# One list of steps for the seven-product blocks and the down projection of a feed-forward block

## The chip, the cores and the metric

The kernel runs on one core of one Trainium2 chip. The metric is device time in microseconds (us) of one execution; three executions of the kernel before gave 2733.2, 2736.87 and 2738.81 us, median 2736.87. A further execution was profiled; the rows below are of that one.

## The reference

The program is one hybrid layer (dilated attention beside a gated linear recurrence) followed by a block of two layers, each made of a feed-forward block, a token mixer and a second feed-forward block, over 512 tokens of width 1024. Everything is float32. What the change touches is a feed-forward block:

```python
D_MODEL, SEQ, D_FF = 1024, 512, 2816
def _swiglu(h, w_gate, w_up, w_down):
    return (jax.nn.silu(h @ w_gate) * (h @ w_up)) @ w_down
...
h = _rmsnorm(x, norm_g[l, 0]) * (1.0 + sc0) + sh0
x = x + 0.5 * g0 * _swiglu(h, ffn_w_gate[l, 0], ffn_w_up[l, 0], ffn_w_down[l, 0])
```

There are four such blocks. The first one is computed by another function (`ffn`), the other three by `ffn7`, so the change touches three stages of the program.

## The kernel before

All float32 products are made of three products of parts: `split` (L390 to L400) writes the rounded high half of an operand on ScalarE (ACT, L399) and the rest, the low half, on VectorE (DVE, L400); TensorE (PE) then multiplies high by high, low by high and high by low.

In `ffn7`, the 22 column blocks (of 128) of the hidden width are taken in pairs. The first two pairs of blocks (0 to 3) are computed in the plain way. The other nine pairs (blocks 4 to 21) use seven products where the plain way has eight: gate and up weights of 256 columns, each cut into two halves of 512 rows, are a two by two matrix of pieces A11, A12 (gate), A21, A22 (up); the normed input, cut by rows and by tokens, is the other one. In the code A11 and A12 are the two halves of a `raw` tile, A21 and A22 are `pc` tiles. Each product (`prod`) is 24 matmuls at L1385, each with 256 columns. In order the seven are called here by their second operand: b11 and b21 (in `begin`), then t2, t1, t3, b22 and t4 (in `rest`). b11, t2, t3 and t4 add up in one PSUM bank (`acc`), which ScalarE copies out in between (L1399, L1417, L1427); t1 and b22 share another bank (`att`), which is copied out once (L1424).

Three of the left operands are sums that VectorE makes first, in place: A21+A22 in two halves (L1411), A21+A11 (L1412), A11 plus the first sum (L1414, in two halves) and A12 plus that (L1428). t2 multiplies what L1414 left in the `raw` tile, so its split needs both of them done. When all products of a pair are there, L1436 to L1441 make the activation (tanh on ScalarE, products and halves) into `sm` and `pT` tiles, and `down` multiplies the activations of two pairs with four column parts of the down weights (L1454, 24 matmuls of 512 columns for each part) and adds them to x (L1259).

A block runs `begin` of the first pair, `down` of the pass before, `rest`, and then `begin` and `rest` of the second pair with no `down` between. The passes are blocks 4 to 7, 8 to 11, 12 to 15, then 16 and 17 alone (one pair, and its `down` half as long), then 18 to 21, whose down projection is in `tail`. So in each of the three stages there are four places where a pair's `begin` is followed at once by its `rest`: pairs 6, 10, 14 and 20.

What sets the order: each engine has a list of instructions that it runs one after the other. A scheduler lays the lists out before the run, from the dependencies, from the order in which the program issues the work (earlier first) and from when tiles come free. `hi` and `lo` have 4 buffers each, `raw` 2, the pieces (`piece`, L1336) 3, the accumulators `acc` 2 and `att` 6. Loads are issued on SyncE's queue (SP).

Of the kernel before, what the change touches and what calls it, by code (L numbers as in the profile page):

```python
# [8 lines left out]
F32 = mybir.dt.float32  # L9
# [285 lines left out]
class Prog:  # L295
# [1047 lines left out]
    def ffn7(self, l, s, h, nxt):  # L1343
# [44 lines left out]
        class Pair:  # L1388
            pass

        def begin(f):

            u = Pair()
            u.cs = slice(f * 128, f * 128 + 256)
            u.raw = self.wload([(0, wg[:, u.cs])], KD, 256)
            u.a = self.acc()
            prod(u.a, both(u.raw[:, 0:4, :]), forms.b11, True)
            u.s1 = self.s()
            nc.scalar.activation(u.s1, u.a, AF.Copy)  # L1399
            b = self.att()  # L1400
            prod(b, both(u.raw[:, 4:8, :]), forms.b21, True)
            nc.vector.tensor_add(u.s1, u.s1, b)
            return u

        def rest(u, dst):
            u.p21, u.p22 = (self.piece(wu[a:a + 512, u.cs], 4) for a in (0, 512))
            a11, a12 = u.raw[:, 0:4, :], u.raw[:, 4:8, :]

            s1 = [self.s(shape=(128, 2, 256)) for _ in range(2)]
            for i in range(2):  # L1410
                nc.vector.tensor_add(s1[i], u.p21[:, 2 * i:2 * i + 2, :], u.p22[:, 2 * i:2 * i + 2, :])  # L1411
            nc.vector.tensor_add(u.p21, u.p21, a11)  # L1412
            for i in range(2):
                nc.vector.tensor_add(a11[:, 2 * i:2 * i + 2, :], a11[:, 2 * i:2 * i + 2, :], s1[i])  # L1414
            prod(u.a, both(a11), forms.t2, False)
            s2 = self.s()
            nc.scalar.activation(s2, u.a, AF.Copy)  # L1417
            c = self.att()
            hi, lo = (self.wp.tile([128, 4, 256], F32R, name=self.nm(n), tag=n) for n in ("hi", "lo"))
            for i in range(2):  # L1420
                self.split(s1[i], hi[:, 2 * i:2 * i + 2, :], lo[:, 2 * i:2 * i + 2, :])
            prod(c, (hi, lo), forms.t1, True)
            s5 = self.s()
            nc.scalar.activation(s5, c, AF.Copy)  # L1424
            prod(u.a, both(u.p21), forms.t3, False)
            s3 = self.s()
            nc.scalar.activation(s3, u.a, AF.Copy)  # L1427
            nc.vector.tensor_add(a12, a12, a11)  # L1428
            prod(c, both(a12), forms.b22, False)
            nc.vector.tensor_add(s3, s3, s5)  # L1430
            nc.vector.tensor_add(s2, s2, c)
            prod(u.a, both(u.p22), forms.t4, False)

            for hf, (g, up) in enumerate(((u.s1, u.a), (s2, s3))):
                t = self.s()
                nc.scalar.activation(t, g, AF.Tanh, scale=0.5)  # L1436
                nc.vector.scalar_tensor_tensor(t, t, 1.0, g, op0=ALU.add, op1=ALU.mult)
                nc.vector.tensor_mul(t, t, up)
                hi, lo = (d[:, hf].rearrange("p f n -> p (f n)") for d in dst)
                nc.scalar.activation(hi, t, AF.Copy, scale=-1.0)  # L1440
                nc.vector.scalar_tensor_tensor(lo, t, -1.0, hi.bitcast(F32), op0=ALU.mult, op1=ALU.subtract)  # L1441

        def down(f0, f1, aa):
            kc = f1 - f0
            for p in range(4):
                raw = self.piece(wd[f0 * 128:f1 * 128, p * 256:(p + 1) * 256], kc)
                hi, lo = (self.wp.tile([128, 4, 256], F32R, name=self.nm(n), tag=n)[:, 0:kc, :] for n in ("hi", "lo"))
# [660 lines left out]
```

## Time and profile before

| | |
|---|---|
| median of three executions | 2736.87 us |
| the profiled execution | 2743.27 us |
| its span, first to last instruction | 2741.5 us |
| mean granted TensorE clock | 0.986 of full speed |
| PE busy | 2625.5 us, 96% |
| DVE busy | 1978.6 us, 72% |
| ACT busy | 1168.8 us, 43% |

The profiled execution is 6.4 us (0.2%) above the median. Its time lies 1.8 us above its span. Busy means that an instruction of the engine was under way. A row of the chain, of the waits or of the time line says in the last place who ended the wait.

### The profile page before, as it was taken

Reading aid. Unit: us, or ns where it says so; the run is one execution under the profiler, and the core shown is the slowest. Engines: PE = TensorE matmul, PEld = TensorE weight load, DVE = VectorE, ACT = ScalarE, POOL = GpSimd, SP = SyncE. Lnnn points to the kernel's source line nnn. Section 1 sums busy time; section 2 is a strip of 40 time slices with the busy share of each in tenths; the row PEclk is TensorE's granted clock in tenths of the full one; section 3 lists DMA queues with packets and bytes.
Section 4 is the critical chain, followed back from the end, with each engine's and each line's share of the span. In section 5 each row is a group of like instructions: output and inputs, shape, how many; then the busy total and the mean of one; then the engine's idle time right before and its main releaser. Section 6 shows DMA issues by size and latency. Waiting matters only on the chain.

```text
span 2741.5 us, 40806 instructions
## 1 busy us (share of the span) xinstructions
PE 2625.5 (96%) x15952; PEld 2289.4 (84%) x15952; DVE 1978.6 (72%) x3401; ACT 1168.8 (43%) x2112; POOL 321.6 (12%) x425
## 2 busy tenths in 40 slices
PE   7999989999998999999999999999999999999998
PEld 6878767788787889887888888888889887888888
DVE  8776874845887546788777777777777688667776
ACT  5332342624322224547534435444444547434434
POOL 4010010103000002423200001000002413200001
PEclk9999999999999999999999999999999999999999
DMA  9867645232676333622133334133233522123321
GB/s 273 248 199 219 215 141 182 65 122 93 199 232 223 118 104 103 180 67 62 55 93 94 105 94 133 52 93 100 85 116 98 168 57 66 58 89 106 99 84 63
DMA packets 317233, 339.70 MB, mean 124 GB/s; under 512 B 22128, under 2 KB 287856, under 8 KB 317040
## 3 DMA queue, kind: packets, MB, share of 16 engines
q1 hardware_dynamic: 317040, 337.10, 40.4%
q8 instruction: 125, 2.05, 0.3%
q14 instruction: 68, 0.56, 0.1%
HBM read 328.67 MB, written 8.39 MB: 123 GB/s over the span
## 4 chain that ended last, share of the span: by engine, by line
PE 72%; DVE 12%; DMA 9%; issue 3%; ACT 2%; POOL 1%; SPq 0%; DVEq 0%; POOLq 0%; ACTq 0%
PE acc L1385 11%; PE att L1454 10%; PE att L1385 8%; DMA mraw<-in_w_ada 8%; PE acc L417 6%; PE acc L419 6%; PE acc L415 5%; DVE macc L656 3%; PE acc L467 2%; PE acc L573 2%; PE acc L577 2%; DVE lo L400 2%; PE acc L575 2%; PE att L1895 1%; PE att L1879 1%
## 5 line engine op out<-in xcount | busy, mean ns | idle before, releaser
L399 ACT ACTIVATE hi<-raw 128x1024 fp32r<-128x1024 f32 (+2 forms) x329 | 326.7, 994 | 484.9 <-PE acc L419 134.7
L400 DVE TENSOR_TENSOR lo<-raw,hi 128x1024 fp32r<-128x1024 f32 (+2 forms) x329 | 379.1, 1154 | 107.8 <-ACT hi L399 103.6
L1385 PE MATMUL acc<-s,hi 128*128 128x256 f32 x1728 | 261.0, 286 | 31.2 <-ACT hi L399 31.2
L415 PE MATMUL acc<-s,hi 128*128 128x512 f32 x1008 | 274.4, 407 | 15.8 <-ACT s L399 7.9
L417 PE MATMUL acc<-s,lo 128*128 128x512 f32 x1008 | 266.7, 400 | 0.0
L1385 PEld LDWEIGHTS acc<-s,hi 128*128 128x128 f32 x1728 | 233.2, 194 | 35.2 <-ACT hi L399 33.6
L419 PE MATMUL acc<-s,hi 128*128 128x512 f32 x1008 | 260.8, 395 | 0.0
L130 POOL TENSOR_TENSOR q<-q,q 128x256 f32<-128x256 f32 x96 | 79.8, 832 | 1531.3 <-ACT q L125 1529.4
L656 DVE SCALAR_TENSOR_TENSOR macc<-mraw,cs,macc 128x1024 f32<-128x1024 f32 x133 | 171.0, 1286 | 106.5 <-DMA mraw<-in_w_ada 102.7
L415 PEld LDWEIGHTS acc<-s,hi 128*128 128x128 f32 x1008 | 190.4, 192 | 62.2 <-ACT s L399 9.1
L417 PEld LDWEIGHTS acc<-s,lo 128*128 128x128 f32 x1008 | 192.4, 191 | 45.9 <-issue 0.5
L419 PEld LDWEIGHTS acc<-s,hi 128*128 128x128 f32 x1008 | 190.1, 189 | 43.7
L400 DVE TENSOR_TENSOR lo<-pc,hi 128x1024 fp32r<-128x1024 f32 (+1 forms) x138 | 156.3, 1134 | 80.0 <-ACT hi L399 79.7
L1385 PE MATMUL att<-s,hi 128*128 128x256 f32 x1296 | 197.1, 284 | 0.1
L399 ACT ACTIVATE hi<-pc 128x1024 fp32r<-128x1024 f32 (+1 forms) x138 | 135.1, 981 | 108.3 <-PE att L1454 52.9
L1385 PEld LDWEIGHTS att<-s,hi 128*128 128x128 f32 x1296 | 172.6, 191 | 1.6 <-ACT hi L399 1.6
L1454 PE MATMUL att<-sm,hi 128*128 128x512 f32 x528 | 146.4, 393 | 0.0
L1385 PE MATMUL acc<-s,lo 128*128 128x256 f32 x864 | 141.4, 287 | 4.3 <-DVE lo L400 4.3
L1259 DVE SCALAR_TENSOR_TENSOR x<-att,der,x 128x512 f32<-128x512 f32 x120 | 89.6, 749 | 66.8 <-PE att L1454 66.8
L1259 DVE SCALAR_TENSOR_TENSOR x<-acc,der,x 128x256 f32<-128x256 f32 (+1 forms) x136 | 76.0, 560 | 73.9 <-PE acc L577 48.8
L1385 PEld LDWEIGHTS acc<-s,lo 128*128 128x128 f32 x864 | 121.1, 194 | 4.9 <-DVE lo L400 4.9
L1454 PEld LDWEIGHTS att<-sm,hi 128*128 128x128 f32 x528 | 98.5, 188 | 22.3
(493 smaller groups left out, 5484.5 us busy)
## 6 DMA issues: line engine op xcount, KB each, us to landing
mraw<-in_w_ada SPq DMA_DIRECT2D x144, 512.0 KB, 4.3
raw<-in_ffn_w_gate SPq DMA_DIRECT2D x44, 1024.0 KB, 5.4
raw<-in_w_in SPq DMA_DIRECT2D x30, 1024.0 KB, 6.2
pc<-in_ffn_w_up SPq DMA_DIRECT2D x60, 512.0 KB, 3.8
pc<-in_ffn_w_down SPq DMA_DIRECT2D x60, 512.0 KB, 3.6
raw<-in_w_in SPq DMA_DIRECT2D x46, 512.0 KB, 5.3
raw<-in_ffn_w_up SPq DMA_DIRECT2D x14, 1024.0 KB, 6.9
raw<-in_ffn_w_down SPq DMA_DIRECT2D x12, 768.0 KB, 5.7
```

The costliest lines, as they stand in the source:

```text
L130: nc.gpsimd.tensor_tensor(parts[-1], parts[-1], sq, op=ALU.add)
L399: self.nc.scalar.activation(hi, src, AF.Copy)
L400: self.nc.vector.tensor_sub(lo, src, hi.bitcast(F32))
L415: mm(ps, hi[:, k, :], xh[k], start=(k == 0), stop=False)
L417: mm(ps, lo[:, k, :], xh[k], start=False, stop=False)
L419: self.last_mm = mm(ps, hi[:, k, :], xl[k], start=False, stop=(k == kc - 1)).ins
L467: self.last_mm = mm(ps, x[k][:, ts], ws[k // 4][part][:, k % 4, :], start=(i == 0 and k == 0), stop=(i == 2 and k == KD - 1)).ins
L573: mm(ps, hi[k], ah[k], start=(k == 0), stop=False)
L656: nc.vector.scalar_tensor_tensor(st["acc"], raw, cs[:, k:k + 1], st["acc"], op0=ALU.mult, op1=ALU.add)
L1259: self.nc.vector.scalar_tensor_tensor(x, ps, gate[:, c:c + 1], x, op0=ALU.mult, op1=ALU.add)
L1385: mm(o, a[:, k, cs], b[k], start=(first and f == i == k == 0), stop=(last and i == 2 and k == 3), skip_group_check=True)
L1454: mm(ps.rearrange("p (a n) -> p a n", a=2), w[:, k, cs], aa[k // 2][x][:, :, k % 2, :], start=(i == k == 0), stop=(i == 2 and k == kc - 1))
```

## The change

`begin`, `rest` and `down` become lists of steps. A step has three parts: its loads, its split (with the sums that the split needs), and its products with what follows them. The seven products of a pair are seven steps, each part of `down` one. The steps of a pass are put in the order in which `ffn7` ran its products before: two of the first pair, the four of the earlier `down`, the other five, then seven of the second pair. A loop then issues, at each turn n, the loads of step n+6, the split of step n+3 and the products of step n. The two halves of the activation change places (second half first), and the add of t1's copy to t3's stands right behind t3's copy. The pools and their buffers stay as they are. Lines of the new kernel: copies L1434, sums L1410 to L1413 and L1417, adds L1444, L1458 and L1462, activation L1470 to L1475, down L1504.

```diff
-        def begin(f):
...
-            prod(u.a, both(u.raw[:, 0:4, :]), forms.b11, True)
...
-        def rest(u, dst):
-            u.p21, u.p22 = (self.piece(wu[a:a + 512, u.cs], 4) for a in (0, 512))
...
-            prod(u.a, both(a11), forms.t2, False)
...
+            def sums():
+
+                p21, p22 = u["u"]
+                u["s1"] = [self.s(shape=(128, 2, 256)) for _ in range(2)]
+                for i in range(2):
+                    nc.vector.tensor_add(u["s1"][i], p21[:, 2 * i:2 * i + 2, :], p22[:, 2 * i:2 * i + 2, :])
+                nc.vector.tensor_add(p21, p21, a1(0))
+                for i in range(2):
+                    nc.vector.tensor_add(a1(0)[:, 2 * i:2 * i + 2, :], a1(0)[:, 2 * i:2 * i + 2, :], u["s1"][i])
...
+            def whole(key, src, before=None):
+                def g():
+                    if before:
+                        before()
+                    u[key] = parts()
+                    self.split(src(), *u[key])
+                return g
...
+            def run3():
+                prod(u["c"], u["S4"], forms.b22, False)
+                nc.vector.tensor_add(u["p2"], u["p2"], u["c"])
+
+            def run4():
+                prod(u["a"], u["A22"], forms.t4, False)
+
+                aa = dst()
+                for hf, (g, up) in ((1, (u["p2"], u["p3"])), (0, (u["p1"], u["a"]))):
...
+            no = lambda: None
+            return [(load_g, whole("A11", lambda: a1(0)), run1), (no, whole("A12", lambda: a1(1)), run2),
+                    (load_u, whole("S2", lambda: a1(0), sums), run6), (no, split1, run5),
+                    (no, whole("S3", lambda: u["u"][0]), run7), (no, whole("S4", lambda: a1(1), sum4), run3),
+                    (no, whole("A22", lambda: u["u"][1]), run4)]
...
-        u = begin(4)
-        down(0, 4, aa)
+        steps, before = [], down(0, 4, aa)
         for f0, f1 in ((4, 8), (8, 12), (12, 16), (16, 18), (18, 22)):
             aa = []
...
+            new = []
             for f in range(f0, f1, 2):
-                aa.append(a_tiles())
-                rest(u, aa[-1])
-                u = begin(f + 2) if f + 2 < 22 else None
-            if f1 < 22:
-                down(f0, f1, aa)
+                new += seven(f, dst)
+
+            steps += new[0:2] + before + new[2:]
+            before = down(f0, f1, aa)
+        ahead = 3
+        for n in range(-2 * ahead, len(steps)):
+            for st, k in enumerate((n + 2 * ahead, n + ahead, n)):
+                if 0 <= k < len(steps):
+                    steps[k][st]()
```

First place, VectorE between pair 4 and pair 6 of a stage, before. `raw_12791` is the second pair's gate weights, `pc_12856` and `pc_12858` its up weights, `s_12860` and `s_12861` the sums; the L1438 and L1441 rows finish the first pair's activation, and `att_12824` is the bank of the second pair's b21.

```order
L1438 TENSOR_TENSOR s_12785<-s_12785,s_12718 128x512
L1438 TENSOR_TENSOR s_12779<-s_12779,acc_12417 128x512
L1441 SCALAR_TENSOR_TENSOR sm_12615<-s_12785,sm_12614 128x512
L1441 SCALAR_TENSOR_TENSOR sm_12615<-s_12779,sm_12614 128x512
L1411 TENSOR_TENSOR s_12860<-pc_12856,pc_12858 128x512
L1411 TENSOR_TENSOR s_12861<-pc_12856,pc_12858 128x512
L1412 TENSOR_TENSOR pc_12856<-pc_12856,raw_12791 128x1024
L1414 TENSOR_TENSOR raw_12791<-raw_12791,s_12860 128x512
L1402 TENSOR_TENSOR s_12822<-s_12822,att_12824 128x512
L1414 TENSOR_TENSOR raw_12791<-raw_12791,s_12861 128x512
L1428 TENSOR_TENSOR raw_12791<-raw_12791 128x1024
L400 TENSOR_TENSOR lo_12868<-raw_12791,hi_12867 128x1024
```

The same place after. `raw_12607`, `pc_12672` and `pc_12674` are the second pair's weights, `s_12767` and `s_12768` the sums; L1458 adds t1's copy to t3's copy of the first pair, L1462 adds the bank of its b22, and L1471 and L1472 begin its activation.

```order
L1410 TENSOR_TENSOR s_12767<-pc_12672,pc_12674 128x512
L1458 TENSOR_TENSOR s_12735<-s_12735,s_12705 128x512
L1410 TENSOR_TENSOR s_12768<-pc_12672,pc_12674 128x512
L400 TENSOR_TENSOR lo_12739<-raw_12607,hi_12738 128x1024
L1462 TENSOR_TENSOR s_12670<-s_12670,att_12680 128x512
L1411 TENSOR_TENSOR pc_12672<-pc_12672,raw_12607 128x1024
L1471 SCALAR_TENSOR_TENSOR s_12804<-s_12804,s_12670 128x512
L1413 TENSOR_TENSOR raw_12607<-raw_12607,s_12767 128x512
L1413 TENSOR_TENSOR raw_12607<-raw_12607,s_12768 128x512
L1472 TENSOR_TENSOR s_12804<-s_12804,s_12735 128x512
L1471 SCALAR_TENSOR_TENSOR s_12810<-s_12810,s_12470 128x512
L400 TENSOR_TENSOR lo_12775<-raw_12607,hi_12774 128x1024
```

The sums of the second pair stood behind the whole activation of the first pair, the second of the L1414 rows also behind L1402, which needs the second pair's b21. Now they stand before the first pair's last product is used, mixed with the start of its activation, and both adds of banks that stand ahead of them belong to the first pair.

ScalarE at the same place, before (L1436 is tanh, L1440 the activation's high half, L1399 the copy of the second pair's b11 out of its bank):

```order
L1436 ACTIVATE s_12785<-s_12655 128x512
L1440 ACTIVATE sm_12614<-s_12785 128x512
L1440 ACTIVATE sm_12614<-s_12779 128x512
L1399 ACTIVATE s_12822<-acc_12793 128x512
L399 ACTIVATE hi_12867<-raw_12791 128x1024
```

And after (L1470 is tanh, L1474 the activation's high half, L1434 the copy of the second pair's b11 out of its bank):

```order
L1470 ACTIVATE s_12804<-s_12670 128x512
L1470 ACTIVATE s_12810<-s_12470 128x512
L399 ACTIVATE hi_12774<-raw_12607 128x1024
L1474 ACTIVATE sm_12802<-s_12804 128x512
L399 ACTIVATE hi_12816<-s_12767 128x512
L399 ACTIVATE hi_12816<-s_12768 128x512
L1434 ACTIVATE s_12847<-acc_12822 128x512
```

The high half of t2's operand (`hi_12774`) stood behind both activation halves and behind the copy of b11; now it stands ahead of them, behind the two tanh.

Second place, VectorE during the half-long `down` of the pass with blocks 16 and 17, before (`raw_14639` is the gate weights of pair 18; L1259 adds `down`'s banks to x):

```order
L1414 TENSOR_TENSOR raw_14639<-raw_14639,s_14797 128x512
L1259 SCALAR_TENSOR_TENSOR x_93<-att_14760,der_8730,x_93 128x512
L1428 TENSOR_TENSOR raw_14639<-raw_14639 128x1024
L1259 SCALAR_TENSOR_TENSOR x_94<-att_14774,der_8730,x_94 128x512
L1259 SCALAR_TENSOR_TENSOR x_95<-att_14782,der_8730,x_95 128x512
L400 TENSOR_TENSOR lo_14804<-raw_14639,hi_14803 128x1024
```

The same place after, with `raw_14455` for `raw_14639`:

```order
L1413 TENSOR_TENSOR raw_14455<-raw_14455,s_14747 128x512
L1259 SCALAR_TENSOR_TENSOR x_92<-att_14779,der_8730,x_92 128x512
L1259 SCALAR_TENSOR_TENSOR x_93<-att_14787,der_8730,x_93 128x512
L400 TENSOR_TENSOR lo_14754<-raw_14455,hi_14753 128x1024
L400 TENSOR_TENSOR lo_14774<-s_14746,hi_14773 128x512
L400 TENSOR_TENSOR lo_14774<-s_14747,hi_14773 128x512
L400 TENSOR_TENSOR lo_14798<-pc_14661,hi_14797 128x1024
L1259 SCALAR_TENSOR_TENSOR x_94<-att_14801,der_8730,x_94 128x512
L1259 SCALAR_TENSOR_TENSOR x_95<-att_14809,der_8730,x_95 128x512
```

The low half of t2's operand stood behind the last two updates of x, which wait for the last part of `down`, and behind L1428; now it stands ahead of them.

On every engine the same instructions stand as before (3285 rows of VectorE's list, 13587 of TensorE's); SP's list of loads reads the same row for row. In TensorE's list the only rows that move in the seven-product blocks are the first four matmuls of t1 at 12 places, which the scheduler had put among t2's; in `tail` the first products of two banks are interleaved in another way.

## Rows read from the trace of the kernel before

**Rows 1.** The page, busy time by engine: us, share of the span, instructions.
```profile
PE 2625.5 (96%) x15952; PEld 2289.4 (84%) x15952; DVE 1978.6 (72%) x3401; ACT 1168.8 (43%) x2112; POOL 321.6 (12%) x425
```

**Rows 2.** One stage: length, busy us of PE, PEld, DVE, ACT, POOL; clock; DMA.
```profile
1385.80:1681.30 295.50, 283.70 (x1943) 263.39 (x1942) 219.19 (x264) 123.49 (x164) 0.00 (x0) 0.99 0.32 97
```

**Rows 3.** L1385 in the three stages: ns min/median/max, first and last start.
```profile
L1385 PE MATMUL acc<-s,hi x576: 277/281/582, 1385.5 to 1681.2; 128*128 128x256 f32 x192
L1385 PE MATMUL acc<-s,hi x576: 277/281/419, 1757.7 to 2055.3; 128*128 128x256 f32 x192
L1385 PE MATMUL acc<-s,hi x576: 276/280/581, 2408.6 to 2704.9; 128*128 128x256 f32 x192
```

**Rows 4.** Time line of PE around pair 6: start, us, [idle before, releaser].
```profile
1424.76 0.64 PE L1385 MATMUL acc<-s,hi 128*128 128x256 f32 x4
...
1430.45 0.64 PE L1385 MATMUL att<-s,hi 128*128 128x256 f32 x4
...
1436.04 0.78 PE L1385 MATMUL acc<-s,hi 128*128 128x256 f32 x4 [2.60 <-ACT hi L399]
```

**Rows 5.** The chain that ended last, a whole down projection: start, us.
```profile
1391.34 22.22 PE att L1454 x96
```

**Rows 6.** Waits of PE, whole span: us in total, times, longest.
```profile
PE acc L1385 <- ACT hi L399: 31.2, 12, 2.6
...
PE acc L1385 <- DVE lo L400: 4.3, 3, 1.5
```

**Rows 7.** Time line of VectorE around pair 6.
```profile
1430.06 1.29 DVE L1411 TENSOR_TENSOR s<-pc,pc 128x512 f32<-128x512 f32 x2
1431.38 1.23 DVE L1412 TENSOR_TENSOR pc<-pc,raw 128x1024 f32<-128x1024 f32 x1
1432.64 0.69 DVE L1414 TENSOR_TENSOR raw<-raw,s 128x512 f32<-128x512 f32 x1
1433.55 0.69 DVE L1402 TENSOR_TENSOR s<-s,att 128x512 f32<-128x512 f32 x1 [0.21 <-PE att L1385]
1434.15 0.69 DVE L1414 TENSOR_TENSOR raw<-raw,s 128x512 f32<-128x512 f32 x1
1434.87 1.23 DVE L1428 TENSOR_TENSOR raw<-raw 128x1024 f32<-128x1024 f32 x1
1436.02 1.23 DVE L400 TENSOR_TENSOR lo<-raw,hi 128x1024 fp32r<-128x1024 f32 x1
```

**Rows 8.** Time line of ScalarE around pair 6.
```profile
1430.65 0.60 ACT L1399 ACTIVATE s<-acc 128x512 f32<-128x512 f32 x1 [1.24 <-PE acc L1385]
1434.93 1.06 ACT L399 ACTIVATE hi<-raw 128x1024 fp32r<-128x1024 f32 x1 [3.68 <-DVE raw L1414]
1435.89 1.14 ACT L399 ACTIVATE hi<-s 128x512 fp32r<-128x512 f32 x2
```

**Rows 9.** The 5 us behind a restart, columns as in rows 2.
```profile
1436.04:1441.04 5.00, 5.00 (x28) 4.98 (x29) 4.68 (x6) 2.89 (x4) 0.00 (x0) 0.66 0.05 10
1502.54:1507.54 5.00, 4.98 (x39) 4.78 (x40) 4.68 (x6) 3.94 (x6) 0.00 (x0) 1.00 0.08 9
...
2689.30:2694.30 5.00, 5.00 (x29) 5.00 (x30) 4.68 (x6) 2.88 (x4) 0.00 (x0) 0.66 0.06 10
```

**Rows 10.** Time line of VectorE at pair 18.
```profile
1633.24 0.69 DVE L1411 TENSOR_TENSOR s<-pc,pc 128x512 f32<-128x512 f32 x1 [0.67 <-DMA pc<-in_ffn_w_up]
...
1639.43 0.75 DVE L1259 SCALAR_TENSOR_TENSOR x<-att,der,x 128x512 f32<-128x512 f32 x1
...
1641.22 1.41 DVE L1259 SCALAR_TENSOR_TENSOR x<-att,der,x 128x512 f32<-128x512 f32 x2
```

**Rows 11.** Time line of PE at pair 18.
```profile
1641.36 0.64 PE L1385 MATMUL acc<-s,hi 128*128 128x256 f32 x4
...
1643.81 0.74 PE L1385 MATMUL acc<-s,lo 128*128 128x256 f32 x4 [1.35 <-DVE lo L400]
```

**Rows 12.** Waits of ScalarE in the first stage (1337 to 1700 us).
```profile
ACT hi L399 <- DVE raw L1414: 30.7, 6, 8.5
```

More of the change, by code (lines that the diff above doesn't have):

```diff
@@ L1386, in prod @@
                            skip_group_check=True)
-        class Pair:
-            pass
-        def begin(f):
[L1393 to L1396, printed above, removed]
-            prod(u.a, both(u.raw[:, 0:4, :]), forms.b11, True)
[L1398 to L1403, printed above, removed]
@@ L1405, in rest @@
-        def rest(u, dst):
-            u.p21, u.p22 = (self.piece(wu[a:a + 512, u.cs], 4) for a in (0, 512))
[L1407 to L1414, printed above, removed]
-            prod(u.a, both(a11), forms.t2, False)
[L1416 to L1441, printed above, removed]
@@ L1443, in down, with load, split, run @@
         def down(f0, f1, aa):
             kc = f1 - f0
+            out = []
             for p in range(4):
-                raw = self.piece(wd[f0 * 128:f1 * 128, p * 256:(p + 1) * 256], kc)
-                hi, lo = (self.wp.tile([128, 4, 256], F32R, name=self.nm(n), tag=n)[:, 0:kc, :] for n in ("hi", "lo"))
-                self.split(raw, hi, lo)
-                for m in range(2):
-                    cs = slice(m * 128, m * 128 + 128)
-                    ps = self.att()
-                    for i, (w, x) in enumerate(((hi, 0), (lo, 0), (hi, 1))):
-                        for k in range(kc):
-                            mm(ps.rearrange("p (a n) -> p a n", a=2), w[:, k, cs], aa[k // 2][x][:, :, k % 2, :],
-                               start=(i == k == 0), stop=(i == 2 and k == kc - 1))
-                    upd(p * 2 + m, full, ps)
+                u = {}
+                def load(u=u, p=p):
+                    u["w"] = self.piece(wd[f0 * 128:f1 * 128, p * 256:(p + 1) * 256], kc)
+                def split(u=u):
+                    u["p"] = [t[:, 0:kc, :] for t in parts()]
+                    self.split(u["w"], *u["p"])
+                def run(u=u, p=p):
+                    hi, lo = u["p"]
+                    for m in range(2):
+                        cs = slice(m * 128, m * 128 + 128)
+                        ps = self.att()
+                        for i, (w, x) in enumerate(((hi, 0), (lo, 0), (hi, 1))):
+                            for k in range(kc):
+                                mm(ps.rearrange("p (a n) -> p a n", a=2), w[:, k, cs], aa[k // 2][x][:, :, k % 2, :],
+                                   start=(i == k == 0), stop=(i == 2 and k == kc - 1))
+                        upd(p * 2 + m, full, ps)
+                out.append((load, split, run))
@@ L1459, in ffn7 @@
+            return out
         got = []
@@ L1483, in ffn7, with dst @@
         forms.over()
-        u = begin(4)
-        down(0, 4, aa)
         i = 3 * l + s + 1
+        steps, before = [], down(0, 4, aa)
         for f0, f1 in ((4, 8), (8, 12), (12, 16), (16, 18), (18, 22)):
             aa = []
+            def dst(aa=aa):
+                aa.append(a_tiles())
+                return aa[-1]
+            new = []
             for f in range(f0, f1, 2):
-                aa.append(a_tiles())
-                rest(u, aa[-1])
-                u = begin(f + 2) if f + 2 < 22 else None
-            if f1 < 22:
-                down(f0, f1, aa)
+                new += seven(f, dst)
[6 more added lines that the diff above has]
+                    steps[k][st]()
         prep = None
```

46 lines of the change are left out of this document (added).

## Prediction, made before the changed kernel had run

> **What bounds the kernel now.** I read the page's busy times first. TensorE (PE) is under way for 96% of the span, VectorE for 72% [rows 1], so PE is the engine to follow, and the change can only pay where PE stands still or runs slowly inside the three stages that `ffn7` makes. The stretch view of the first of them shows 283.70 us of PE in 295.50, VectorE 219.19 [rows 2].
>
> Next I compared the length of each stage with its work. From the first L1385 start to the last the stages take 295.7, 297.6 and 296.3 us [rows 3], with the last matmul 889.9 us in all. The work goes by undisturbed stretches. Between 1424.76 and 1430.45 PE starts 48 matmuls, two whole products [rows 4]: 5.69 / 48 = 118.5 ns each, 2.84 us for a product of 24. A whole `down` takes 22.22 us [rows 5]. A stage has nine pairs of seven products, 1512 matmuls, 179.2 us, and four and a half `down`s, 100.0 us: 279.2 us, three times that 837.6. So 52.3 us of the three stages are lost, and that is all that a better order can win there.
>
> Where they go stands in the list of PE's waits: 12 waits of L1385 for ScalarE's high half, 31.2 us, none longer than 2.6, and 3 for a low half, 4.3 us [rows 6]. The 12 are the four places in each stage where a pair's first two products are followed at once by its t2. The time line shows one: t2 starts at 1436.04, behind 2.60 us of idle [rows 4]. ScalarE wrote its high half from 1434.93, behind 3.68 us of waiting for VectorE's L1414 [rows 8]. VectorE in turn came to the sums (L1411) only at 1430.06 and, with L1402 between (it waits for the b21 of the same pair), to the second L1414 at 1434.15 [rows 7]. It had no idle time to speak of: the sums stand too late in its list.
>
> The idle time has a second price. In the 5 us from 1436.04 PE's granted clock is 0.66 of full speed, so part of them ran at 1.2 instead of 2.4 GHz, with 28 matmuls recorded; behind an equal wait, from 1502.54, it is 1.00, with 39 [rows 9]. Of the 12 places 8 look like the first row (0.66 to 0.69, the first and the last are shown), 4 like the second. The 8 lose about 0.33 of 5 us, 1.65 us each, 13.2 in all.
>
> Here the Trainium skill bears on the reading ("Trainium Kernel Development and Optimization", Performance Expectations): matmul busy time says little of how close a kernel is to its limit, because matmuls are pipelined. The trace agrees: PE is busy 5.00 of 5.00 us at the clock of 0.66 [rows 9]. By busy time alone a stage loses 295.50 - 283.70 = 11.8 us, 35 in three; by the starts of matmuls it is 52.
>
> **The change part by part.** No instruction is removed or added, and SP's list of loads reads the same. So there is no cost per instruction, and "loads six steps ahead" moves nothing by itself: with three piece buffers a load goes when a split frees one, before as after. I take 0 for the loads, with both ends near 0, since the splits that free the buffers come no later.
>
> *The 12 places.* In the new list of VectorE the second pair's sums stand between the first pair's adds, ahead of the end of its t4. I work the chain out from T = 0, the end of the first pair's b22. PE then has that pair's t4 and the second pair's b11 and b21 to do: t2 is reached at 3 x 2.84 = 8.5. For the steps I take the distances of starts in the trace: 0.60 us for a 128x512 row of VectorE (1433.55 to 1434.15), 1.15 for a 128x1024 row (1434.87 to 1436.02) [rows 7], on ScalarE 0.96 for a 128x1024 high half and 0.60 for a copy [rows 8].
> The rows ahead of L1462 come from t3's end at -2.84: t3's copy until -2.0, L1458, one L1410 and A12's low half until +0.4 (0.60 + 0.60 + 1.15). Then L1462 until 1.0, L1411 until 2.15, L1471 until 2.75 (its tanh ran on ScalarE from 1.1 to 1.75), two L1413 until 4.0. ScalarE writes the high half from 4.1 to 5.2, wanted at 8.5: 3.3 us to spare. VectorE goes on with L1472 and L1471 until 5.2 and writes the low half until 6.4; PE wants it four matmuls after t2's start, at 9.0: 2.6 to spare. ScalarE then has one activation half (0.6), t1's two high halves (1.1) and the copy of b11 (0.6): 7.4. t2 adds into the bank that this copy reads, so the copy must be done at 8.5: 1.1 to spare, the least of all.
> Further on: t1's low halves are done at about 8.8, wanted at 11.4 and 0.5 later; t3's at 10.6, wanted at 14.2; L1417, behind L1444, at 12.4, and with its high and low half b22's operand at 14.6, wanted at 17.0. What is late next is thus nothing by the chain; behind VectorE's L1462, which waits for b22, stand the sums, and behind them ScalarE and PE, which is why the chain had to be counted. If the cover went, every us beyond 8.5 would cost 12 us and some clock.
> So I take the waits to go whole: 31.2 us of idle and 13.2 of clock. Bounds: nothing won (all stays, if the chain takes 8.5 + 2.6 us; with more it is a loss, which is a rival below), and 52.3 - 4.3 = 48 us from above, since a matmul list without waits can't be shorter than its spacing.
>
> *The 3 low halves.* At pair 18 the sums begin late, at 1633.24, when the up weights have landed; the sixth update of x stands at 1639.43, and the low half waited until the last two updates (1641.22, 1.41 us) were through [rows 10], so PE stood 1.35 us [rows 11]. In the new list the low half stands ahead of those two and of L1428, right behind the sixth update: from about 1640.1 to 1641.3. PE wants it at 1641.36 + 4 x 0.1185 = 1641.8. I take the 4.3 us [rows 6] as won; ends 0 and 4.3 (0.5 us of room is not much).
>
> *The activation halves.* The second half comes first now. `down` uses them two products later, so this is hidden there. In `tail` the first half is wanted at once. At worst it comes later by what is put ahead of it, a multiply of 0.60 and a high half of 0.96, 1.6 us in each of three stages; at best the earlier sums bring it forward by as much. PE's list interleaves two banks there, so I take 0 and keep -5 and +5 us.
>
> *Sum.* 31.2 + 13.2 + 4.3 = 48.7 by the waits, 52.3 by stage length less work. I take 50 us. Against the profiled execution: 2743.27 - 50 = 2693. That execution lay 6.4 us above the median, so for the median of three: 2736.87 - 50 = 2687.
>
> **The rivals.**
>
> *A short wait stays at each place.* The room for b11's copy is 1.1 us and each hand-over between engines can cost more than I put in. If PE stands 1.35 us, as at pair 18 [rows 11], at 12 places, 16 us are left: 2703; with the half clock behind 8 of them 29 us: 2716. For it: ScalarE has four rows to do between the sums and that copy. Against it: no step of the chain is without room.
>
> *The waits stay, because they come from buffers.* A gap of 2.60 us that recurs 12 times could come from tiles that have no free buffer, `hi` and `lo` having four; the change leaves these counts alone, so the time would stay at 2737. Against it: ScalarE's high halves waited 30.7 us for VectorE's L1414 in the first stage [rows 12], so for data, not for PE to release a buffer. The Trainium skill has this as a rule ("Perfetto Trace Analysis", Optimization Strategy): the same gap repeating on the engine that should be saturated can mean that there isn't enough memory for the next tile. By that rule the time is 2737; the trace speaks against it here, by the row just named.
>
> *Slower: the chain through L1462.* In the new lists ScalarE has two tanh ahead of t2's high half, the first of them waits for VectorE's L1462, and that for PE's b22; before, the sums hung on no product of the first pair. If this chain took longer than the 8.5 us of cover plus the 4 us that a place loses now, 12.5 us from b22's end, the kernel would be slower. At 14 us each place costs 5.5 idle and 1.65 clock, 86 us in 12, less the 50: 2773. For it: ScalarE has waited up to 8.5 us for L1414 [rows 12]. Against it: the counted chain takes 5.2 us, less than half.
>
> *The change doesn't do what it says.* For the loads this is so (their list is unchanged), and it is in the sum with 0. For the splits the lists show the move.
>
> **How the numbers follow.** Forecast (2687, own range 2679 to 2697, by a gain of 52.3 + 5 at one end and of 48.7 - 4.3 - 5 at the other): 0.76. A short wait (2703 to 2716): 0.15. Buffers, or no change for another reason (2737): 0.05. Slower (2773): 0.04. The range of 8 in 10 is 2678 to 2711: it holds the forecast's case with what it may win in `tail`, and most of the short waits. About 0.2%, 5.5 us, is what a measurement of this kernel can tell from no change; only the third case lies in there. Faster 0.91, same 0.05, slower 0.04.
>
> **What would show it.** Right: PE's list of waits has no 12 waits of L1385 for a high half, the clock is 1.00 all through the three stages, each of which takes 279 to 281 us from its first L1385 to its last; L1410 stands before b21 of its own pair, and t2 follows b21 in 0.12 us. The low-half wait at pair 18 is gone or under 0.5 us. Wrong: waits of t2 for ScalarE's copy L1434 or for a low half, stages of 285 us or more, or stages as forecast with the time coming back in `tail` (L573 waiting longer than before) or behind it. A time over 2711 would mean that the chain from L1462 was counted too short; one under 2678, that something outside these three stages moved too.

## The result, and the profile after

The changed kernel takes 2694.6 us (median of 4 runs, 2693.8 to 2695.1), beside 2737.8 for the kernel before in the same set (2733.2 to 2743.8). The ratio is 0.9841, interval 0.9821 to 0.9860. The forecast was 2687 with a range of 2678 to 2711.

The profiled execution took 2695.07 us, its span is 2693.3, against 2743.27 and 2741.5 before: 48.2 us less. The page's line of busy times, which answers to [rows 1], gives PE 20 us less busy time for the same 15952 matmuls:

```profile
PE 2605.3 (97%) x15952; PEld 2275.8 (85%) x15952; DVE 1973.2 (73%) x3401; ACT 1165.9 (43%) x2112; POOL 322.5 (12%) x425
```

The same group of L1385 in the three stages, as in [rows 3]: ns min/median/max, first and last start.

```profile
L1385 PE MATMUL acc<-s,hi x576: 277/281/287, 1387.0 to 1666.0; 128*128 128x256 f32 x192
L1385 PE MATMUL acc<-s,hi x576: 277/281/287, 1742.4 to 2021.4; 128*128 128x256 f32 x192
L1385 PE MATMUL acc<-s,hi x576: 276/280/287, 2376.6 to 2654.3; 128*128 128x256 f32 x192
```

Read it by its ends and by the third duration. The stages take 279.0, 279.0 and 277.7 us, together 53.9 less than before. The longest matmul is 287 ns where it was 419 to 582, so none of them ran at half clock. The list of PE's waits has no row of L1385 any more. The first stage as one stretch (columns as in [rows 2]) shows PE busy from end to end at a granted clock of 1.00:

```profile
1387.20:1666.20 279.00, 279.00 (x1945) 260.13 (x1945) 217.63 (x265) 122.49 (x164) 0.00 (x0) 1.00 0.32 103
```

Around pair 6, where t2 had started at 1436.04 behind 2.60 us of idle [rows 4], the time lines of PE, VectorE and ScalarE now read as follows (start, us, idle before and releaser):

```profile
1425.83 0.64 PE L1385 MATMUL att<-s,hi 128*128 128x256 f32 x4
...
1434.36 0.63 PE L1385 MATMUL att<-s,hi 128*128 128x256 f32 x4
1434.83 0.64 PE L1385 MATMUL acc<-s,hi 128*128 128x256 f32 x4
1435.30 0.64 PE L1385 MATMUL acc<-s,lo 128*128 128x256 f32 x4
```

```profile
1426.63 0.68 DVE L1462 TENSOR_TENSOR s<-s,att 128x512 f32<-128x512 f32 x1
1427.22 1.22 DVE L1411 TENSOR_TENSOR pc<-pc,raw 128x1024 f32<-128x1024 f32 x1
1428.36 0.68 DVE L1471 SCALAR_TENSOR_TENSOR s<-s,s 128x512 f32<-128x512 f32 x1
1428.96 1.28 DVE L1413 TENSOR_TENSOR raw<-raw,s 128x512 f32<-128x512 f32 x2
...
1431.46 1.23 DVE L400 TENSOR_TENSOR lo<-raw,hi 128x1024 fp32r<-128x1024 f32 x1
```

```profile
1427.34 1.16 ACT L1470 ACTIVATE s<-s 128x512 f32<-128x512 f32 x2 [2.14 <-DVE s L1462]
1430.36 1.06 ACT L399 ACTIVATE hi<-raw 128x1024 fp32r<-128x1024 f32 x1 [1.87 <-DVE raw L1413]
1431.33 0.62 ACT L1474 ACTIVATE sm<-s 128x512 fp32r<-128x512 f32 x1
1431.85 1.14 ACT L399 ACTIVATE hi<-s 128x512 fp32r<-128x512 f32 x2
1432.89 0.58 ACT L1434 ACTIVATE s<-acc 128x512 f32<-128x512 f32 x1
```

t2 (1434.83) follows b21 (last row 1434.36, four matmuls) without idle. Its high half is written from 1430.36, 4.5 us ahead of it, behind the sums (L1413, done at 1430.24) and both tanh. ScalarE's wait for VectorE is still 1.87 us here; but it now lies under PE's products and costs nothing.

Outside the three stages 5.7 us came back: the first stage starts 1.5 later (in work that the change doesn't touch), the way from the second to the third stage takes 355.2 instead of 353.3, and what follows the last L1385 takes 39.0 instead of 36.5 (last start of L1385 to the end of the span). The last two hold `tail`. PE's waits in `tail` for the activation (of L573 for the second multiply and for the high half) were 0.90 and 1.27, 0.88 and 1.45, 2.00 and 0.16 us: 6.7 in all. Before they were 1.98 and 0.16, 1.12 and 0.16, 0.55 and 0.43: 4.4. In the list of PE's waits (us, times, longest), before and then after, nearly all of the rise is in the wait for the high half:

```profile
PE acc L573 <- DVE s L1438: 3.6, 3, 2.0
...
PE acc L573 <- ACT sm L1440: 0.8, 3, 0.4
```

```profile
PE acc L573 <- DVE s L1472: 3.8, 3, 2.0
...
PE acc L573 <- ACT sm L1474: 2.9, 3, 1.5
```

The stretch of 15 us from the last L1385 of each stage on, before and then after (columns as in [rows 2]), shows the second part of that price:

```profile
1681.18:1696.18 15.00, 11.71 (x93) 10.90 (x92) 13.12 (x22) 8.76 (x17) 4.71 (x5) 1.00 0.68 198
2055.29:2070.29 15.00, 12.65 (x100) 11.81 (x99) 12.31 (x21) 8.64 (x17) 4.90 (x6) 1.00 0.42 121
2704.92:2719.92 15.00, 14.02 (x115) 13.43 (x114) 8.06 (x15) 5.44 (x11) 4.43 (x6) 1.00 0.00 1
```

```profile
1666.00:1681.00 15.00, 11.72 (x94) 10.92 (x93) 13.49 (x22) 9.25 (x18) 4.88 (x5) 1.00 0.61 190
2021.40:2036.40 15.00, 11.62 (x82) 11.01 (x81) 12.85 (x21) 8.81 (x17) 3.81 (x4) 0.89 0.26 80
2654.30:2669.30 15.00, 12.61 (x90) 12.00 (x89) 7.79 (x15) 4.75 (x9) 3.44 (x5) 0.89 0.00 0
```

The clock was 1.00 in all three `tail`s; now it is 0.89 in two, so some matmuls there ran at 1.2 instead of 2.4 GHz. 0.11 of 15 us is 1.65 us in each (an estimate from these rows), and the matmul counts fall with it (100 to 82, 115 to 90). Why the activation is late shows in ScalarE's time line ahead of the last `tail`:

```profile
2652.08 1.06 ACT L399 ACTIVATE hi<-pc 128x1024 fp32r<-128x1024 f32 x1 [1.47 <-DMA pc<-in_ffn_w_down]
2653.05 1.13 ACT L1470 ACTIVATE s<-s 128x512 f32<-128x512 f32 x2
2655.20 1.06 ACT L399 ACTIVATE hi<-pc 128x1024 fp32r<-128x1024 f32 x1 [1.01 <-DMA pc<-in_ffn_w_down]
2656.24 1.23 ACT L1474 ACTIVATE sm<-s 128x512 fp32r<-128x512 f32 x2
```

The two tanh (L1470) stand behind the high half of a weight piece that waits 1.47 us for its load, and the activation's own high halves (L1474) behind another that waits 1.01.

### The profile page after: what moved, and what is told of

Its sections match the earlier page's. It is cut to its first block, busy times and chain, and to the rows that moved or that the text cites. A ratio compares the mean times of both kernels' runs of the same rounds, so it can differ in the third digit from the quotient of the medians.

```text
span 2693.3 us, 40840 instructions
## 1 busy us (share of the span) xinstructions
PE 2605.3 (97%) x15952; PEld 2275.8 (85%) x15952; DVE 1973.2 (73%) x3401; ACT 1165.9 (43%) x2112; POOL 322.5 (12%) x425
## 4 chain that ended last, share of the span: by engine, by line
PE 70%; DVE 13%; DMA 10%; issue 4%; ACT 2%; POOL 1%; SPq 0%; DVEq 0%; POOLq 0%; ACTq 0%
PE att L1504 10%; PE acc L1385 9%; DMA mraw<-in_w_ada 8%; PE att L1385 7%; PE acc L417 6%; PE acc L415 6%; PE acc L419 6%; DVE lo L400 3%; DVE macc L656 2%; PE acc L467 2%; PE acc L573 2%; PE acc L575 2%; PE acc L577 2%; PE att L1955 2%; PE att L1939 1%
## 5 line engine op out<-in xcount | busy, mean ns | idle before, releaser
L1385 PE MATMUL acc<-s,hi 128*128 128x256 f32 x1728 | 253.1, 281 | 0.0
L415 PEld LDWEIGHTS acc<-s,hi 128*128 128x128 f32 x1008 | 188.8, 191 | 61.5 <-ACT s L399 8.6
L1385 PEld LDWEIGHTS acc<-s,hi 128*128 128x128 f32 x1728 | 226.4, 189 | 1.5
L419 PEld LDWEIGHTS acc<-s,hi 128*128 128x128 f32 x1008 | 189.9, 189 | 43.6
L1385 PE MATMUL att<-s,hi 128*128 128x256 f32 x1296 | 192.5, 281 | 0.0
L1385 PEld LDWEIGHTS att<-s,hi 128*128 128x128 f32 x1296 | 169.9, 189 | 0.0
L1504 PE MATMUL att<-sm,hi 128*128 128x512 f32 x528 | 146.4, 393 | 0.0
L1259 DVE SCALAR_TENSOR_TENSOR x<-att,der,x 128x512 f32<-128x512 f32 x120 | 88.5, 748 | 67.6 <-PE att L1504 67.5
L1385 PE MATMUL acc<-s,lo 128*128 128x256 f32 x864 | 137.1, 280 | 0.0
L1259 DVE SCALAR_TENSOR_TENSOR x<-acc,der,x 128x256 f32<-128x256 f32 (+1 forms) x136 | 75.8, 560 | 77.3 <-PE acc L577 52.1
L1385 PEld LDWEIGHTS acc<-s,lo 128*128 128x128 f32 x864 | 117.3, 188 | 0.0
L1504 PEld LDWEIGHTS att<-sm,hi 128*128 128x128 f32 x528 | 98.5, 188 | 22.2
```

The costliest lines, as they stand in the source:

```text
L415: mm(ps, hi[:, k, :], xh[k], start=(k == 0), stop=False)
L419: self.last_mm = mm(ps, hi[:, k, :], xl[k], start=False, stop=(k == kc - 1)).ins
L1259: self.nc.vector.scalar_tensor_tensor(x, ps, gate[:, c:c + 1], x, op0=ALU.mult, op1=ALU.add)
L1385: mm(o, a[:, k, cs], b[k], start=(first and f == i == k == 0), stop=(last and i == 2 and k == 3), skip_group_check=True)
L1504: mm(ps.rearrange("p (a n) -> p a n", a=2), w[:, k, cs], aa[k // 2][x][:, :, k % 2, :], start=(i == k == 0), stop=(i == 2 and k == kc - 1))
```

## The experiments

Each set below ran on one chip with runs of the kernel before beside it; times are medians. Since executions differ by several us ahead of the first stage (last section), I also give the time from the first L1385 to the end of the span, called *the stages' part*: 1356.0 us before, 1306.3 after.

Two theories stood at the start. A: the time was lost because the second pair's sums stood in VectorE's list behind the first pair's activation and, in part, behind a product of their own pair; moving the splits far enough ahead moves them past that. B: it is the list of steps, or the loads, that helps.

**The kernel before, again.** No edit.

> The kernel before once more, for its spread. Theory A (the clock part of a wait comes or not from one execution to the next): its 12 waits of L1385 for a high half are 2.6 us each in every execution, 31 us, but the number of them followed by a stretch at half clock differs from the 8 of 12 in the profiled execution; executions lie between 2733 and 2744 us, and the quicker ones have the higher mean clock, about 1.65 us for each place. Theory B (the spread comes from somewhere else): again 8 of 12, and the mean clock does not go with the time.

2748.19 us (ratio 1.0005, 0.9988 to 1.0021), from 2739.8 to 2750.6; the 2733 to 2744 that I expected was too low. The profile has the 12 waits of 2.60 us again, and 9 of the 12 stretches of 5 us behind them at a clock of 0.66 to 0.70 where the first profile had 8. Two of them, one of each kind:

```profile
1435.38:1440.38 5.00, 4.97 (x26) 4.77 (x27) 4.68 (x6) 2.88 (x4) 0.00 (x0) 0.66 0.05 11
...
1877.97:1882.97 5.00, 4.98 (x39) 4.78 (x40) 4.68 (x6) 3.96 (x6) 0.00 (x0) 1.00 0.07 14
```

So the wait belongs to the program and is the same to 0.01 us each time; the clock behind it is not.

**The list, without running ahead.**

```
-        ahead = 3
-        for n in range(-2 * ahead, len(steps)):
-            for st, k in enumerate((n + 2 * ahead, n + ahead, n)):
+        for n in range(-6, len(steps)):
+            for st, k in enumerate((n + 6, n + 0, n)):
```

> The changed kernel with its list of steps and loads six steps ahead, but each split and its sums issued directly before the products that use them. Theory A (the sums again stand behind the first pair's activation in VectorE's list): the 12 waits of about 2.6 us are back, also half clock at some of them, 2733 to 2744 us. Theory B (the list itself, or the loads issued six steps ahead, make the difference): 2694 to 2700 us.

2749.88 us, ratio 1.0012 (0.9993 to 1.0030). PE's waits, as in [rows 6] (us, times, longest):

```profile
PE acc L1385 <- ACT hi L399: 31.2, 12, 2.6
PE acc L1385 <- DVE lo L400: 4.4, 3, 1.5
```

The list of steps and the loads six ahead are worth nothing alone.

**Splits two steps ahead.** As above with `n + 2` for the splits.

> The changed kernel with splits two steps ahead instead of three. Then only the two halves of the first sum stand ahead of the end of the first pair's activation in VectorE's list, the other sums behind it, and the add of b21 behind the sums. Theory A (each row on that list ahead of t2's high half counts with its time): about 2.0 us of the 2.6 go (two rows of 0.6, one of 0.6 and its wait), so 12 waits of about 0.6 us or none stay, little half clock, 2694 to 2706 us. Theory B (it is the lookahead of three steps as such): waits near 2.6 us stay, 2730 us or more.

2733.92 us, ratio 0.9949 (0.9935 to 0.9962): a gain of 13 us where theory A had more. The waits of PE, and two of the 12 stretches of 5 us from a restart:

```profile
PE acc L1385 <- ACT hi L399: 10.6, 12, 1.0
...
PE acc L573 <- DVE s L1472: 9.5, 3, 4.2
PE acc L1385 <- DVE lo L400: 8.3, 12, 0.7
```

```profile
1439.03:1444.03 5.00, 4.28 (x21) 3.88 (x22) 5.00 (x6) 2.88 (x4) 0.00 (x0) 0.70 0.00 0
1504.88:1509.88 5.00, 4.27 (x31) 3.87 (x32) 5.00 (x6) 2.97 (x5) 0.00 (x0) 1.00 0.00 0
```

At two steps most of the sums stand behind the first pair's activation rows, but ahead of the add that takes up b21 of their own pair. The wait at each place falls from 2.6 to 0.9 for the high half, and a new one of 0.7 for the low half stands behind it; at 4 of the 12 places the clock falls all the same (0.70 to 0.74). The third stage is 290.7 us against 296.3 in the run before and 277.8 at three steps: two thirds of the loss stay. The direction of theory A holds, its size did not: I had counted one wait per place and no clock. The listed waits (18.9 us) and the low clock at the 4 places (about 6 us, by the shares of 5 us) make up about 25 of the 35 us by which the three stages are longer than at three steps; the rest isn't accounted for.

**The sums alone, ahead of the activation.** In the kernel before, the second pair's sums are issued ahead of the first pair's activation, but with its first two products ahead of both. So the edit does more than its expectation says: the first pair's activation also goes behind the second pair's b11 and b21.

```
...
-                rest(u, aa[-1])
+                if f == f0:
+                    sums(u)
+                act2 = rest(u, aa[-1])
                 u = begin(f + 2) if f + 2 < 22 else None
+                if f + 2 < f1:
+                    sums(u)
+                act2()
```

> The kernel before with one thing moved: the loads and sums of a second pair are issued ahead of the first pair's activation; the splits stay where they were, and there is no list of steps. Theory A (the place of the sums in VectorE's list is all): the 12 waits for a high half go, the 3 low-half waits at pair 18 (4.3 us) stay, 2697 to 2704 us. Theory B (splits three steps ahead are needed): waits of 1 us or more stay at most of the 12 places, 2715 us or more.

2793.67 us beside 2747.29 before, ratio 1.0180 (1.0151 to 1.0210): slower, which neither theory expected. ScalarE and VectorE at pair 6 (in this kernel L1399 copies b11, L1439 is tanh, L1440 the activation's first multiply, L1410 to L1413 the sums):

```profile
1435.36 0.60 ACT L1399 ACTIVATE s<-acc 128x512 f32<-128x512 f32 x1 [7.00 <-PE acc L1385]
1435.85 1.14 ACT L1439 ACTIVATE s<-s 128x512 f32<-128x512 f32 x2
1440.23 1.06 ACT L399 ACTIVATE hi<-raw 128x1024 fp32r<-128x1024 f32 x1 [3.24 <-DVE raw L1413]
```

```profile
1430.27 1.29 DVE L1410 TENSOR_TENSOR s<-pc,pc 128x512 f32<-128x512 f32 x2
1436.51 0.69 DVE L1440 SCALAR_TENSOR_TENSOR s<-s,s 128x512 f32<-128x512 f32 x1 [4.95 <-ACT s L1439]
1437.12 1.22 DVE L1411 TENSOR_TENSOR pc<-pc,raw 128x1024 f32<-128x1024 f32 x1
```

Both tanh now stand behind the copy of b11 on ScalarE, which waits 7.00 us for PE. VectorE reaches the first half of the sums at 1430.27, and then stands 4.95 us, because the activation's multiply, which waits for that tanh, got into its list ahead of L1411. t2 starts behind 3.19 us of idle instead of 2.60, and the clock behind it is 0.54 (0.54 to 0.58 over 7 us at the four places of the first stage; over 5 us, at all twelve places of the three stages, 0.50 to 0.68):

```profile
1441.34:1448.34 7.00, 7.00 (x34) 6.89 (x35) 6.49 (x8) 3.67 (x6) 0.00 (x0) 0.54 0.06 13
```

This is the prediction's slower rival in another place: a row that hangs on a late product got ahead of the sums. So the place of the sums alone doesn't decide; what counts is what every row ahead of them, on both engines, waits for.

**Sums and the split of A11, ahead of the activation; the products behind it.** If that reading is right, one edit in the kernel before has to give nearly all of the gain, without list or lookahead. (In this cut of the code and in the one for `tail` below, what stands behind # is an explanation.)

```
             prod(u.a, both(u.p22), forms.t4, False)
+            if then:
+                then()    # loads, split of A11 and sums of the next pair
             for hf, (g, up) in enumerate(((u.s1, u.a), (s2, s3))):
...
-                u = begin(f + 2) if f + 2 < 22 else None
+                if u:
+                    begin(u)    # only b11 and b21 and what follows them
```

> The kernel before, with one edit: the second pair's loads, the split of its A11 and its sums are issued ahead of the first pair's activation, while its first two products stay behind that activation (so both tanh stay ahead of the copy of b11 on ScalarE, unlike in the run with the sums alone). No list of steps, the other splits where they were. Theory A (what the place of the sums and the rows ahead of them wait for decides, not how far the splits run ahead in general): the 12 waits of 2.6 us are gone, the 3 low-half waits at pair 18 stay (4 to 5 us), time 1 to 10 us above the changed kernel, ratio 0.983 to 0.989. Theory B (the distance of three steps for every split is what helps): waits of 1 us or more stay at the 12 places, ratio 0.993 or above.

2697.51 us, ratio 0.9828 (0.9805 to 0.9850), beside 2694.96 and 0.9820 (0.9799 to 0.9841) for the changed kernel in the same set. The 12 waits are gone, the 3 of pair 18 stay:

```profile
PE acc L573 <- DVE s L1445: 3.9, 3, 1.9
PE acc L1385 <- DVE lo L400: 3.6, 3, 1.2
```

The stages' part is 1309.1 us, against 1308.6 for the changed kernel in this set: of the 1356.0 us before, this one move takes 47 off. Theory A, in the form that the run before gave it, is shown, and B has fallen: the list and the early loads without the move gave nothing, the move without the list gave nearly all.

**The changed kernel again,** in two sets, for the others to be compared with.

> The changed kernel once more, beside the others of this set. Both theories expect a ratio of 0.982 to 0.986 to the kernel before, no wait of L1385 for a high half, and stages of 278 to 280 us; its `tail` waits (L573 for the second multiply and for the activation's high half) should come to 6 to 7 us over three stages, as in the first profile, against 4.4 before.

> The changed kernel once more, for the other three of this set: ratio to the kernel before 0.982 to 0.986. From the first L1385 to the end of the span 1306 to 1309 us, as in the two profiles so far.

2694.96 us beside 2743.92 before (ratio 0.9820), and 2698.10 beside 2748.10 (0.9826, 0.9807 to 0.9845): 49.0 and 50.0 us. Stages' part 1308.6 and 1306.0. A low-half wait of 0.42 us at pair 18 showed once. The `tail` waits were 7.1 and 8.0 us, the clock behind the stages 0.89 in five of six `tail`s.

**Splits four steps ahead, loads eight.**

> The changed kernel with the splits four steps ahead of the products and the loads eight. Theory A (at three steps the sums stand ahead of the first pair's activation in the list, and nothing waits there any more): no wait to win, stages of 277 to 280 us, time within 3 us of the changed kernel of this set. Rival (the room at three steps is short, as the 0.4 us low-half wait at pair 18 in the second profile of the changed kernel shows, and more distance is worth something): 3 us faster or more. Other rival (four buffers of each half are too few for four steps): waits of ScalarE for TensorE to release a half, 5 us slower or more.

2694.00 us, ratio 0.9809 (0.9789 to 0.9829), 4 us under the changed kernel of its set with intervals that overlap; third stage 278.1 us against 277.8, no wait of L1385. At three steps nothing is left to win in the three stages (their sum is 835.8 us in both), and four buffers carry four steps. But the stages' part is 1302.7 us against 1306.0, so by the time theory A (within 3 us) was missed and the rival's 3 us are reached. The 3.3 us lie outside the three stages: the clock of the three `tail`s is 1.00, 1.00 and 0.89 here, 0.89, 1.00 and 0.89 in the changed kernel of the set. Whether the distance or chance gave that, one profile of each can't say.

**The activation's first half first,** in two sets.

```
-                for hf, (g, up) in ((1, (u["p2"], u["p3"])), (0, (u["p1"], u["a"]))):
+                for hf, (g, up) in ((0, (u["p1"], u["a"])), (1, (u["p2"], u["p3"]))):
```

> The changed kernel with the activation's first half issued first again. Theory T (the 5 us lost outside the three stages are lost in `tail`, where the wanted half comes last): L573's waits fall from 6.7 us to 4 to 5, time 1 to 4 us less than the changed kernel of this set. Theory U (ScalarE's row for a weight piece that has not landed stands ahead of the tanh, whichever half comes first): waits stay within 1.5 us of the changed kernel's, time the same within 2 us.

> The activation's first half first, again. Theory T: 2 to 6 us less than the changed kernel of this set, and from the first L1385 to the end of the span 1303 to 1306 us. If the 6 us less of the set before came from its profiled execution's early start alone (1377.9 against 1389.1 us), the time is the same within 2 us.

2688.64 and 2694.52 us, 6.3 and 3.6 under the changed kernel (ratios 0.9804, 0.9778 to 0.9829, and 0.9810, 0.9792 to 0.9828; the intervals overlap with its own). Stages' part 1304.5 and 1305.2. The last `tail` improves: from the last L1385 to the end 36.2 and 36.6 us against 39.1 and 39.2. In the first two, L573 still waits 1.5 to 1.9 us for the activation's high half, which stands behind the high halves of weight pieces on ScalarE; one of these waits 0.67 us for its load in the first `tail` of the first profile. The waits come to 5.9 us in both sets, where theory T had 4 to 5 and the changed kernel had 7.1 and 8.0. So each of theories T and U has a part of it.

**The first half first, and `tail`'s later splits held behind it,** in two sets.

```
+                    if hf == 0:
+                        self.half0 = ins    # the first half's high part
...
+            if p:
+                self.hold = (1, (self.half0, self.half0))    # the split of piece p waits for it
```

> The changed kernel with the first half first and the splits of `tail`'s second to fourth weight pieces held behind the first half's high part, so that no ScalarE row that waits for a load stands ahead of the tanh. Theories T and U both expect L573's waits for the activation at 1 to 3 us in all three stages and 3 to 8 us less than the changed kernel; a rival, that the held splits are then late themselves, expects new waits of L573 for a weight half and no gain.

> First half first and `tail`'s later splits held, again. Theory T: 3 to 7 us less than the changed kernel of this set, from the first L1385 to the end of the span 1301 to 1304 us; the rival (held splits cost what the wait gives) expects the time of the first half first alone, within 1 us.

2691.84 and 2692.98 us, 3.1 and 5.1 under the changed kernel (ratios 0.9806, 0.9784 to 0.9828, and 0.9801, 0.9782 to 0.9821). Stages' part 1302.1 and 1304.7. PE's waits of the second profile:

```profile
PE acc L573 <- DVE x L1259: 4.8, 5, 1.5
...
PE acc L573 <- DVE s L1472: 2.3, 3, 0.9
PE acc L573 <- ACT sm L1474: 1.4, 3, 0.6
```

The waits for the activation fall from 8.0 to 3.7 us, and the clock is 1.00 in five of six `tail`s. A new one comes in: L573 waits 4.8 us for VectorE's updates of x, 2.3 in the changed kernel. This version was below the kernel before and the changed kernel in both sets; the intervals don't separate it from the changed one. Its stages' part in the second set missed the 1301 to 1304 that I expected. Against the first half first alone this version was 3.2 us slower in one set and 1.5 faster in the other, which can't be told from zero.

## Why the prediction was right, and where it was off

*The 12 places: right, to the step.* The counted chain starts at the end of b22, 1426.47 in the time lines above (its last row starts at 1425.83 and takes 0.64). Behind that point (measured at pair 6 of the first stage, with the count in brackets): L1462 done at 0.8 us (1.0), both L1413 at 3.8 (4.0), high half 3.9 to 5.0 (4.1 to 5.2), low half done at 6.2 (6.4), copy of b11 at 7.0 (7.4), t2 at 8.4 (8.5). Every step came 0.1 to 0.4 early, and the least room, ahead of the copy, was 1.4 us instead of 1.1. All 31.2 us of idle went.

*The clock in the stages: right.* 1.00 throughout. 53.9 us were won in the stages where the count by stage length gave 52.3; the work without waits was 277.7 to 279.0 us, I had 279.2. So "all that a better order can win" was 1.6 us too low: the third stage needs 1.3 us less than the other two, which no run explains. The waits and the clock as I had added them (48.7) fell short by 5.2. The clock's 13.2 us rested on one execution with 8 low places; other profiles with the same twelve waits had 9 (the kernel before) and 7 (the list without running ahead).

*The low halves at pair 18: right.* Gone in the first profile; one wait of 0.42 to 0.54 us in three of the later ones that keep these splits (the changed kernel once, and once each of the two versions for `tail`); the 0.5 us of room was as small as I had said.

*`tail`: mis-sized.* I took 0, with ends of -5 and +5; it cost 4.3 us in the profile (1.9 + 2.4). This is the sign of being wrong that the prediction named: stages as forecast, with time coming back in `tail`. The stages' part less the three stages themselves shows it again: 466.4 and 465.5 us in the two profiles of the kernel before, 470.6, 472.2 and 470.2 in those of the changed kernel. I had counted the multiply and the high half that come ahead of the wanted half, but not ScalarE's rows for weight pieces, which stand ahead of them and wait for a load, nor the clock. By the same measure the two experiments on it bring 2 to 4 us back (468.9 and 468.1 with the first half first, 466.5 and 467.8 with the splits held too). Four steps ahead, which leaves `tail`'s order of halves alone, came to 466.9 as well, so how much belongs to the order and how much to whether the clock falls is open.

*From the profile to the median: the step that failed.* The profile's gain was 48.2 us against 50 forecast, 1.8 off; that is in part luck, since 3.9 us more than the 50 were won in the stages and 5.7 came back outside them. The other 5.8 of the 7.6 us between 2687 and 2694.6 come from the step "that execution lay 6.4 us above the median": I took 6.4 off the changed kernel's time as well, but its profiled execution lies only 0.5 above its median. The median of three runs was low: later sets gave 2747.29, 2743.92 and 2748.10 for the kernel before (25, 7 and 9 runs), with 2694.96 and 2698.10 for the changed one in the last two. By those medians the gain is 49.0 and 50.0 us. The sets ran on several chips, so the chip's part in it stays open; the changed kernel's medians, 3.5 us apart over three sets, speak against a large one.

*The rivals.* A short wait didn't stay at the 12 places at three steps, but is just what two steps show. Buffers: refuted, since the one move of sums and a split took the 12 waits away with the same four buffers. The repeating gap that the Trainium skill's page "Perfetto Trace Analysis" (Optimization Strategy) can put down to missing memory was here a matter of order on VectorE and ScalarE; the wait of ScalarE for VectorE's data [rows 12] told it beforehand. The slower chain did not come true in the changed kernel, but the run with the sums alone shows its mechanism at a price of 46 us, with another link (the copy of b11) than the one I had named. The loads did nothing, as said.

## What to carry to other kernels

When an engine that should be full stands still for data, follow the wait through the helpers' lists to the row that stands too late, and count, from the one product that the new order hangs on, each row of each helper until the data is wanted; here that count came out within 0.4 us a step at pair 6 of the first stage. Before moving a row ahead, ask of every row that will stand ahead of it, on both engines, what it waits for: the same sums moved with one copy in front made the kernel 1.8% slower instead of 1.7% faster. And make the sum against the profiled execution, but don't correct it to a median of three runs whose spread (5.6 us) is nearly as large as the correction (6.4).

## What the runs showed of the hardware that was not expected

Behind equal waits TensorE's clock falls at some places and not at others. Behind twelve waits of 2.60 us, alike to 0.01 us, the granted clock of the next 5 us was 0.66 to 0.70 at 8 or 9 places and 1.00 at the others, not at the same ones in the two profiles of the kernel before (pair 20 of the first stage, for one, was low in both, pair 10 only in the second). With waits of 0.9 and 0.7 us it still fell at 4 of 12 places, and behind the twelve of 3.2 to 3.3 us in the run with the sums alone at all of them. Where idle time is removed, the clock's part has to be counted by its granted share, as a number that varies from run to run.

Much of the spread between executions arises in the first 480 us, long before the changed lines. The first L1385 started between 1377.9 and 1392.8 us in the profiles, though no edit touches what comes before it. The stretch from 70 to 480 us in the earliest (first half first) and in the latest (four steps ahead), columns as in [rows 2]:

```profile
70.00:480.00 410.00, 386.42 (x2066) 323.33 (x2065) 298.53 (x516) 136.02 (x208) 28.38 (x28) 0.99 0.62 201
```

```profile
70.00:480.00 410.00, 381.05 (x2013) 319.04 (x2012) 289.48 (x506) 125.87 (x193) 24.84 (x25) 0.96 0.63 198
```

In the same 410 us the first has 53 matmuls more in its records, at a mean clock of 0.99 against 0.96. By these shares (0.03 of 410 us is 12) that is two thirds or more of the 14.9 us between the two starts, an estimate. For an edit behind that point, the time from its first instruction to the end is the steadier measure: 1356.0 and 1356.5 us in the two profiles of the kernel before, and 1306.0 to 1308.6 in the three of the changed kernel, so single profiles tell differences of about 3 us apart and not smaller ones.
